# Branch products that share a weight split between the token halves, and an output projection of seven half products

## The chip, the cores and the metric

The kernel runs on 1 core of one Trainium2 chip. The metric is the device time of one launch in microseconds, the median of the runs.

## The reference

One encoder layer on 1024 tokens of 1024 features, in float32. What matters here is the chain of products behind the attention branches:

```python
proj = h @ w_in                                  # h = RMSNorm(x)
y_gla = rms_norm(o_gla) * silu(g_r) @ w_o_gla    # branch A
y_swa = o_swa @ w_o_swa                          # branch B
merged = sigmoid(gate_a) * y_gla + sigmoid(gate_b) * y_swa
x = x + merged @ w_out
h2 = rms_norm(x)
gate, up = split(h2 @ w_ffn_in)                  # 2 x 2816 features
x = x + (silu(gate) * up) @ w_ffn_out
```

## The kernel before

Activations are kept with features on the 128 partitions and tokens along the free axis. The 1024 features are eight tiles (KT = 8), and the tokens two halves of 512 (s = 0, 1), so a tile is 128x512 (HT = 512). Every float32 operand of a product is split into a high part h (a rounded copy, made by ACT) and a low part l (the difference, made by DVE); a product is three matmuls, wh by xh, wh by xl and wl by xh. `wunit` loads a weight block of 128x512 and splits it. The raw blocks have four buffers, h and l five each.

Some products run in a form with seven half products instead of eight: sums and differences of quarter blocks of the weight (`comb`) meet sums and differences of the activations (sets called 11, T1, T2, 21, T3, 22, T4), and the seven results are shared out over the four quarters of the output. A `product` is then four feature tiles by three matmuls, 12 in all. Where two results are the sum of a common part and something else, the products run one behind the other into the same PSUM bank, and the common part is copied out in between, or loaded in first by an ACT copy.

The stages, in the order of the program: the projections of the input with gated linear attention; windowed attention; PAIRS, twelve pairs of input projection (among them the output gate r and the branch gates ga and gb) of which five products each are left (`second_rest`); branches A and B with the output projection; the FFN's input product in 22 blocks (`ffn_in`); and its output product.

Around the change:

- `prep_a(s, k)` loads tile k of the attention output o and of r, forms o times silu(r) times a gain and splits it; `prep_b(s, k)` loads and splits a tile of branch B. In PAIRS one `prep_a(0, f)` is issued behind the eviction of the T3 product in each of the first eight pairs.
- `branch_a(s)`, `branch_b(s)` and `out_proj(s)` run for one token half at a time. Each output tile is an `hgroup`: two weight blocks are loaded and split, then 24 matmuls go into one bank. The order is branch_a(0), branch_b(0), branch_a(1), out_proj(0), branch_b(1), out_proj(1), so each weight block is loaded and split once per half. Behind branch B the merged tile is split at once (mh, ml).
- `out_proj` adds the input x, puts the sum x1 to DRAM, scales it by the gain (xg) and adds its square to `acc`; `combos` makes the FFN's activation sets from xg; `out_stats` turns `acc` into the factor of the norm.
- The FFN runs seven products of 12 matmuls in each block. The first (11) goes into a bank Y, is copied out as p1 and is followed in Y by product 21. p1 stays on chip; the first four blocks make theirs ahead of all others.

PE's instructions keep the order of the program in these stages (`manual_schedule`); on ACT, DVE and SP the scheduler's model sets the order, and each engine issues in that order.

Of the kernel before, what the change touches and what calls it, by code (L numbers as in the profile page):

```python
# [8 lines left out]
F32 = mybir.dt.float32  # L9
# [5 lines left out]
P = 128  # L15
# [7 lines left out]
NA = 4  # L23
NB = 7
# [8 lines left out]
def body(tc, i, out):  # L33
    nc = tc.nc
    with ExitStack() as root:
# [789 lines left out]
        bt = bs.enter_context(tc.tile_pool(name="bt", bufs=2))  # L825
# [59 lines left out]
        def second_rest(f):  # L885
# [16 lines left out]
            if f < 8:  # L902
                with tc.issue_after(v.ins):
                    prep_a(0, f)
# [8 lines left out]
        oa, ob, mh, ml = {0: [], 1: []}, {}, {}, {}  # L913

        def btile(tag, dt=F32, bufs=None):
            return bt.tile([P, HT], dt, tag=tag, name=nm(tag), bufs=bufs)

        def split_in(pool, o, name, k):
            return xsplit(pool, f"{name}h{k}", f"{name}l{k}", o)

        def prep_a(s, k):
            o = stage()
            nc.sync.dma_start(out=o, in_=scr["o", k, s])
            r = stage()
            nc.sync.dma_start(out=r, in_=scr[f"r{k}", s])
            sg = btile("sg", bufs=1)
            nc.scalar.activation(sg, r, AF.Sigmoid)
            nc.vector.tensor_tensor(r, r, sg, op=ALU.mult)
            nc.vector.scalar_tensor_tensor(o, o, og[:, k % 2:k % 2 + 1], r, op0=ALU.mult, op1=ALU.mult)
            oa[s].append(split_in(bo, o, "oa", k))  # L930
# [23 lines left out]
        YX = {q: [] for q in ("11", "T1", "T2", "21", "22", "T3", "T4")}  # L954

        def bsplit(pool, tag, src):
            h = pool.tile([P, HT], FR, tag=tag + "h", name=nm(tag + "h"))
            l = pool.tile([P, HT], FR, tag=tag + "l", name=nm(tag + "l"))
            nc.scalar.activation(h, src, AF.Copy)
            nc.vector.tensor_tensor(l, src, h.bitcast(F32), op=ALU.subtract)  # L960
            return h, l

        def combos(k, step):

            b11, b12, b21, b22 = xg[k][0], xg[k][1], xg[k + 4][0], xg[k + 4][1]
            if step == 0:
                YX["11"].append(bsplit(big1, f"b11{k}", b11))
                YX["21"].append(bsplit(big1, f"b21{k}", b21))
            elif step == 1:
                nc.vector.tensor_tensor(b12, b12, b11, op=ALU.subtract)  # L970
                YX["T1"].append(bsplit(big4, f"bt1{k}", b12))
                YX["22"].append(bsplit(big2, f"b22{k}", b22))
                nc.vector.tensor_tensor(b22, b22, b12, op=ALU.subtract)
                YX["T2"].append(bsplit(big2, f"bt2{k}", b22))
                nc.vector.tensor_tensor(b11, b22, b11, op=ALU.subtract)
                nc.vector.tensor_tensor(b21, b21, b22, op=ALU.subtract)
            else:
                YX["T3"].append(bsplit(big3, f"bt3{k}", b11))
                YX["T4"].append(bsplit(big3, f"bt4{k}", b21))
        bms = ExitStack()  # L980
        bm = bms.enter_context(tc.tile_pool(name="bm", bufs=1, side="right"))
        bob = bs.enter_context(tc.tile_pool(name="bob", bufs=1))

        def hgroup(w, u0, ah, al):
            b = mmtile()
# [8 lines left out]
        acc = fi.tile([P, T], F32, tag="acc", name="acc2")  # L994
        def prep_b(s):
            ob[s] = []
            for k in range(KT):
                o = stage()
                nc.sync.dma_start(out=o, in_=scr["b", k, s])
                ob[s].append(split_in(bob, o, "ob", k))  # L1000

        def gate(nme, s):
            g = btile(nme[:2])
# [4 lines left out]
        def branch_a(s):  # L1008

            for m in range(KT):  # L1010
                g = gate(f"ga{m}", s)
                y = hgroup(i["w_oa"], m, [v[0] for v in oa[s]], [v[1] for v in oa[s]])
                nc.vector.tensor_tensor(xg[m][s], y, g, op=ALU.mult)

        def branch_b(s, between=None):
            for m in range(KT):
                if between and m == 3:
                    between()
                g = gate(f"gb{m}", s)
                y = hgroup(i["w_ob"], m, [v[0] for v in ob[s]], [v[1] for v in ob[s]])  # L1020
                nc.vector.tensor_tensor(g, y, g, op=ALU.mult)
                nc.vector.tensor_tensor(g, g, xg[m][s], op=ALU.add)
                h = bm.tile([P, HT], FR, tag=f"mh{m}", name=nm("mh"))
                l = bm.tile([P, HT], FR, tag=f"ml{m}", name=nm("ml"))
                nc.scalar.activation(h, g, AF.Copy)
                nc.vector.tensor_tensor(l, g, h.bitcast(F32), op=ALU.subtract)
                mh[m], ml[m] = h, l

        def out_proj(s):
            a = acc[:, s * HT:(s + 1) * HT]  # L1030
            for j, m in enumerate((0, 4, 1, 5, 2, 6, 3, 7)):
                xr = stage()
                nc.sync.dma_start(out=xr, in_=i["xT"][m, s])
                y = hgroup(i["w_out"], m, mh, ml)
                nc.vector.tensor_tensor(xr, y, xr, op=ALU.add)
                d = scratch(f"x1_{m}_{s}")
                nc.sync.dma_start(out=d, in_=xr)
                scr["x1", m, s] = d
                nc.scalar.activation(xg[m][s], xr, AF.Copy, scale=g2[:, m:m + 1])
                sq = a if j == 0 else stage()  # L1040
                nc.scalar.activation(sq, xr, AF.Square)
                if j:
                    nc.vector.tensor_tensor(a, a, sq, op=ALU.add)
                if s and m > 3:
                    combos(m - 4, 1)
# [5 lines left out]

        with tc.manual_schedule(engines={mybir.EngineType.PE}):
            branch_a(0)
            prep_b(0)
            for k in range(KT):
                prep_a(1, k)
            branch_b(0)
            branch_a(1)
            prep_b(1)
            out_proj(0)  # L1060
            branch_b(1, lambda: out_stats(0))
        bs.close()
        bigs = ExitStack()
        big1 = bigs.enter_context(tc.tile_pool(name="big1", bufs=1))
        big4 = bigs.enter_context(tc.tile_pool(name="big4", bufs=1))
        big2 = bigs.enter_context(tc.tile_pool(name="big2", bufs=1))
# [6 lines left out]
        home = {"a": ("01", "11", "21", "31", "41", "51", "61", "71"),  # L1073
                "p1": ("01", "11"), "g0": ("41", "51"), "p5": ("00", "10"), "u2": ("20", "30"),
# [25 lines left out]
        def p11(f):  # L1100
            F = feats[f]
            F.Y = mmtile()
            if f < NB:
                w = wunit(i["w_fi"][f, 0])
            else:
                F.r11 = rload(f, 11)
                w = wsplit(F.r11, 512)
            product(F.Y, w, YX["11"], 4, True, False)
            F.p1 = ctile("a" if f < NA else "p1")
            nc.scalar.copy(F.p1, F.Y)  # L1110

        def p21(f):
            F = feats[f]
            w = wunit(i["w_fi"][f, 1]) if f < NB else wsplit(F.r12, 512)
            product(F.Y, w, YX["21"], 4, False, True)
            F.g0 = gate0(F.Y, "a" if f < NA else "g0")

        def ffn_in(f, between):
            F = feats[f]
            if f < NB:  # L1120
                F.r11 = rload(f, 11)
# [12 lines left out]
            for p, g in between:  # L1134
                p(g)
# [96 lines left out]
        with tc.manual_schedule(engines={mybir.EngineType.PE}):  # L1232
            for k in range(4):
                combos(k, 0)
            out_proj(1)
            bms.close()
            big3 = bigs.enter_context(tc.tile_pool(name="big3", bufs=1))

            for f in range(NA):
                if f == NA - 1:  # L1240
                    out_stats(1)
                p11(f)
            for f in range(NA - 1):
                p21(f)
            for k in range(4):
                combos(k, 2)
# [144 lines left out]
```

## Time and profile before

| | us |
|---|---|
| median of 3 runs | 1661.62 (1661.51 to 1662.61) |
| the profiled execution's own time | 1661.65 |
| its span | 1659.9 |
| PE busy | 1639.9 |
| DVE busy | 1183.5 |
| ACT busy | 894.1 |
| PAIRS, from 600.0 to 764.2 | 164.2 |
| branches and projection, to 1026.2 | 262.0 |
| FFN input, from 1046 to 1445 | 399.0 |

PE is TensorE's matmuls and PEld its weight loads, which overlap; DVE is the vector engine, ACT the scalar engine, SP the queue that issues the DMAs. A row of the timeline gives start, duration, engine, line, operation and output <- inputs, and in brackets the idle time before it with what ended it. A line L71 is line 71 of the kernel. In the rows `st` is a staging buffer, `mm` and `ch` are PSUM banks (four of each), wr, wr2 and ws are raw or combined weight blocks, wh and wl their split parts.

### The profile page before, as it was taken

What the parts mean: (1) busy time and instruction counts of PE and PEld (TensorE: products, weight loads), DVE (VectorE), ACT (ScalarE), POOL (GpSimd) and SP (SyncE); (2) the same over time, 40 slices, a digit from 0 to 9 for tenths busy, and PEclk for the clock granted to TensorE, in tenths of its full rate; (3) what the DMA queues carried; (4) which work ended last, traced back from release to release, by engine and by line L of the source; (5) the groups of instructions that cost most, each with busy time, mean ns of one, the idle gap of its engine ahead of it and who ended that gap; (6) DMA issues with size and microseconds to landing.
All of it is one profiled execution on the core that took longest, in us unless ns stands there. A gap on an engine that the chain in (4) does not pass through costs nothing.

```text
span 1659.9 us, 23330 instructions
## 1 busy us (share of the span) xinstructions
PE 1639.9 (99%) x7740; PEld 1361.7 (82%) x7740; DVE 1183.5 (71%) x2276; ACT 894.1 (54%) x1827; POOL 0.2 (0%) x4
## 2 busy tenths in 40 slices
PE   9999999999999999999999999999999999999999
PEld 7888888887888778888888888888888888888887
DVE  8568787846899677654764569766667767679655
ACT  7456776863988754434554456433344434444442
POOL 0000000000000000000000000000000000000000
PEclk9999999999999999999999999999999999999999
DMA  8856757878543486546764545343234443595533
GB/s 278 293 165 206 238 188 241 270 268 289 186 134 108 127 287 214 189 147 221 218 209 141 189 133 165 115 165 102 89 111 157 152 141 132 193 322 189 146 98 119
DMA packets 185993, 304.37 MB, mean 183 GB/s; under 512 B 21166, under 2 KB 46638, under 8 KB 185872
## 3 DMA queue, kind: packets, MB, share of 16 engines
q1 hardware_dynamic: 185872, 302.88, 55.7%
q8 instruction: 61, 1.00, 0.2%
q14 instruction: 60, 0.49, 0.1%
HBM read 206.33 MB, written 96.47 MB: 182 GB/s over the span
## 4 chain that ended last, share of the span: by engine, by line
PE 84%; DVE 6%; ACT 4%; DMA 4%; issue 2%; SPq 0%; DVEq 0%; ACTq 0%
PE mm L75 29%; PE mm L1209 7%; PE mm L853 7%; PE mm L854 7%; PE mm L855 7%; PE ch L75 7%; PE ch L1209 5%; PE ch L853 3%; PE ch L854 3%; PE ch L855 3%; PE mm L245 3%; PE ch L760 1%; DVE wl L71 1%; DMA st<-r 1%; ACT p L743 1%
## 5 line engine op out<-in xcount | busy, mean ns | idle before, releaser
L832 ACT ACTIVATE wh<-ws 128x512 fp32r<-128x512 f32 x136 | 85.6, 631 | 161.2 <-PE ch L854 68.5
L69 ACT ACTIVATE wh<-wr 128x512 fp32r<-128x512 f32 x190 | 118.3, 627 | 96.3 <-PE mm L75 77.3
L71 DVE TENSOR_TENSOR wl<-wr,wh 128x512 fp32r<-128x512 f32 x190 | 130.1, 686 | 38.1 <-ACT wh L69 35.4
L75 PE MATMUL mm<-wh,xh 128*128 128x512 f32 x320 | 127.3, 398 | 0.1
L75 PE MATMUL mm<-wh,xl 128*128 128x512 f32 x320 | 127.1, 397 | 0.0
L75 PE MATMUL mm<-wl,xh 128*128 128x512 f32 x320 | 126.6, 396 | 0.0
L833 DVE TENSOR_TENSOR wl<-ws,wh 128x512 fp32r<-128x512 f32 x136 | 93.4, 686 | 42.5 <-ACT wh L832 42.5
L832 ACT ACTIVATE wh<-a 128x512 fp32r<-128x512 f32 x66 | 41.7, 632 | 93.1 <-PE mm L1209 43.0
L832 ACT ACTIVATE wh<-wr 128x512 fp32r<-128x512 f32 x64 | 40.4, 631 | 85.5 <-PE ch L854 42.4
L833 DVE TENSOR_TENSOR wl<-a,wh 128x512 fp32r<-128x512 f32 x66 | 45.5, 691 | 43.1 <-ACT wh L832 41.0
L1209 PE MATMUL mm<-hh,wh 128*128 128x512 f32 x176 | 68.6, 390 | 0.7 <-DVE c L1148 0.7
L1209 PE MATMUL mm<-hl,wh 128*128 128x512 f32 x176 | 68.5, 389 | 0.0
L1209 PE MATMUL mm<-hh,wl 128*128 128x512 f32 x176 | 68.5, 389 | 0.0
L75 PEld LDWEIGHTS mm<-wl,xh 128*128 128x128 f32 x320 | 60.2, 188 | 9.8
L75 PEld LDWEIGHTS mm<-wh,xl 128*128 128x128 f32 x320 | 60.2, 188 | 9.7
L75 PEld LDWEIGHTS mm<-wh,xh 128*128 128x128 f32 x320 | 60.3, 188 | 9.4 <-ACT st L220 0.3
L846 DVE TENSOR_TENSOR ws<-wr,wr 128x512 f32<-128x512 f32 x68 | 46.7, 689 | 13.5 <-DMA wr<-in_w_fi_dram 10.3
L1182 DVE TENSOR_TENSOR hl<-hr,hh 128x512 fp32r<-128x512 f32 x77 | 52.8, 687 | 4.2 <-ACT hh L1181 4.2
L1209 PE MATMUL ch<-hh,wh 128*128 128x512 f32 x132 | 51.3, 389 | 0.0
L1209 PE MATMUL ch<-hl,wh 128*128 128x512 f32 x132 | 51.3, 389 | 0.0
L1209 PE MATMUL ch<-hh,wl 128*128 128x512 f32 x132 | 51.3, 389 | 0.0
L1181 ACT ACTIVATE hh<-hr 128x512 fp32r<-128x512 f32 x77 | 47.5, 618 | 6.8 <-PE mm L1209 3.9
(542 smaller groups left out, 4934.9 us busy)
## 6 DMA issues: line engine op xcount, KB each, us to landing
wr<-in_w_fi_dram SPq DMA_DIRECT2D x102, 256.0 KB, 2.9
wr<-in_w_f_dram SPq DMA_DIRECT2D x88, 256.0 KB, 3.5
wh<-wh SPq DMA_DIRECT2D x80, 256.0 KB, 3.0
wl<-wl SPq DMA_DIRECT2D x80, 256.0 KB, 2.9
B<-c SPq DMA_DIRECT2D x44, 256.0 KB, 2.1
T<-st SPq DMA_DIRECT2D x44, 256.0 KB, 2.3
a<-in_w_fo_dram SPq DMA_DIRECT2D x44, 256.0 KB, 5.3
hr<-T SPq DMA_DIRECT2D x44, 256.0 KB, 2.7
```

The costliest lines, as they stand in the source:

```text
L69: nc.scalar.activation(h, raw, AF.Copy)
L71: nc.vector.tensor_tensor(l, raw, h.bitcast(F32), op=ALU.subtract)
L75: nc.tensor.matmul(o, a, b, start=start, stop=stop)
L245: nc.tensor.matmul(Y[q], w[:, c], x, start=f0, stop=f1, skip_group_check=True)
L832: nc.scalar.activation(h, src, AF.Copy)
L833: nc.vector.tensor_tensor(l, src, h.bitcast(F32), op=ALU.subtract)
L853: nc.tensor.matmul(o, h[:, c], x[kk][0], start=start and kk == 0, stop=False, skip_group_check=True)
L854: nc.tensor.matmul(o, h[:, c], x[kk][1], start=False, stop=False, skip_group_check=True)
L855: nc.tensor.matmul(o, l[:, c], x[kk][0], start=False, stop=kk == nk - 1, skip_group_check=True)
L1181: nc.scalar.activation(h, r, AF.Copy)
L1182: nc.vector.tensor_tensor(l, r, h.bitcast(F32), op=ALU.subtract)
L1209: nc.tensor.matmul(ys[m], a[:, c], b, start=f0, stop=f1, skip_group_check=True)
```

## The change

- `both(w, m, x)` replaces `hgroup` in branches A and B: one split of each weight block serves both token halves, 48 matmuls into two banks.
- All 16 `prep_a` move into PAIRS (`PREPS`: one or two per pair), all 16 `prep_b` into branch A.
- The order of output tiles in B is 0, 4, 1, 5, ..., and behind each second one `merge(k)` forms the projection's activation sets (YM) from the merged tiles. The sets live in the buffers S0 to S6, which later hold the FFN's sets (YX).
- The output projection is four pairs of seven half products. `out_first(k)` runs product 11 into a bank, has ACT copy it to pt, and runs product 21 into the same bank. `out_open`, `out_go` and `out_rest` run the other five.
- The FFN's first products of all 22 blocks are made ahead (`fill_p`), three in each `out_rest`, ten behind them. Each result p1 is put to DRAM, and `ffn_in` loads it again and copies it into both of its banks.

PE's order in the output projection, first before (the middle of one output tile; mh and ml are the split merged tiles):

```order
L75 MATMUL mm_2694_11532<-mh_2635_11295,wh_2696_11535 128x512
L75 MATMUL mm_2694_11532<-ml_2636_11296,wh_2696_11535 128x512
L75 MATMUL mm_2694_11532<-mh_2635_11295,wl_2697_11537 128x512
L75 MATMUL mm_2694_11532<-mh_2645_11341,wh_2699_11553 128x512
L75 MATMUL mm_2694_11532<-ml_2646_11342,wh_2699_11553 128x512
L75 MATMUL mm_2694_11532<-mh_2645_11341,wl_2700_11555 128x512
```

and after (the end of product 11 and the start of product 21 in `out_first(0)`; S0 and S3 are sets):

```order
L850 MATMUL mm_2509_10939<-S0h3_2499_10915,wh_2511_10942 128x512
L851 MATMUL mm_2509_10939<-S0l3_2500_10916,wh_2511_10942 128x512
L852 MATMUL mm_2509_10939<-S0h3_2499_10915,wl_2512_10944 128x512
L850 MATMUL mm_2509_10939<-S3h0_2417_10427,wh_2515_10962 128x512
L851 MATMUL mm_2509_10939<-S3l0_2418_10428,wh_2515_10962 128x512
L852 MATMUL mm_2509_10939<-S3h0_2417_10427,wl_2516_10964 128x512
```

In both the bank stays the same where the weight block changes; after, the copy of the bank by ACT (pt) lies between the third and the fourth row, and no other product does.

ACT's queue around these copies (pt), after; wh is a split weight block, st a staging buffer:

```order
L67 ACTIVATE wh_2565_11134<-wr_2564_11132 128x512
L1030 COPY pt_2528_11016<-mm_2524_10997 128x512
L67 ACTIVATE wh_2569_11154<-wr_2568_11152 128x512
L1042 COPY mm_2550_11105<-pt_2513_10958 128x512
L1016 ACTIVATE xg10_9594<-st_2532_11036,g2_389 128x512
L1019 ACTIVATE st_2533_11042<-st_2532_11036 128x512
L829 ACTIVATE wh_2589_11223<-ws_2588_11221 128x512
L1030 COPY pt_2544_11076<-mm_2540_11057 128x512
```

and before, in the same stage:

```order
L69 ACTIVATE wh_2752_11795<-wr_2751_11793 128x512
L1039 ACTIVATE xg11_9502<-st_2716_11636,g2_389 128x512
L1041 ACTIVATE st_2724_11679<-st_2716_11636 128x512
L69 ACTIVATE wh_2755_11813<-wr_2754_11811 128x512
L959 ACTIVATE bt11h_2734_11729<-xg11_9502 128x512
L69 ACTIVATE wh_2767_11857<-wr_2766_11855 128x512
```

Before, ACT has no copy of a bank here; after, one stands right behind a weight split.

SP's queue at a double prep, before (o5 and r5 belong to one `prep_a`, ga is a branch gate that is put to DRAM):

```order
L923 DMA st_2053_8732<-o5_0_513 128x512
L116 DMA ga5_1_8730<-st_2052_8728 128x512
L925 DMA st_2054_8734<-r5_0_8275 128x512
L841 DMA wr_2148_9123<-in_w_f_dram 128x512
L841 DMA wr_2149_9125<-in_w_f_dram 128x512
```

and after:

```order
L920 DMA st_2053_8729<-o5_0_513 128x512
L114 DMA ga5_1_8727<-st_2052_8725 128x512
L922 DMA st_2054_8731<-r5_0_8272 128x512
L920 DMA st_2058_8741<-o6_0_515 128x512
L838 DMA wr_2163_9156<-in_w_f_dram 128x512
L922 DMA st_2059_8743<-r6_0_8401 128x512
L838 DMA wr_2164_9158<-in_w_f_dram 128x512
```

The second prep's two loads stand ahead of and between the next weight loads.

DVE's queue at the end of the projection, after (S are the FFN's sets, the last `wl` rows belong to the blocks that `fill_p` makes behind the last pair):

```order
L1010 TENSOR_TENSOR st_2743_11970<-mm_2697_11748,st_2743_11970 128x512
L782 TENSOR_TENSOR S4l3_2776_12056<-xg30_9598,S4h3_2775_12055 128x512
L782 TENSOR_TENSOR S5l3_2784_12072<-xg71_9607,S5h3_2783_12071 128x512
L782 TENSOR_TENSOR S6l0_2786_12076<-xg40_9600,S6h0_2785_12075 128x512
L1021 TENSOR_TENSOR acc2_9620<-acc2_9620,st_2744_11976 128x512
L782 TENSOR_TENSOR S3l3_2751_12003<-xg70_9606,S3h3_2750_12002 128x512
L782 TENSOR_TENSOR S6l1_2788_12080<-xg50_9602,S6h1_2787_12079 128x512
L993 TENSOR_TENSOR xg70_9606<-xg70_9606,ty_2752_12007 128x512
L782 TENSOR_TENSOR S6l2_2790_12084<-xg60_9604,S6h2_2789_12083 128x512
L69 TENSOR_TENSOR wl_2801_12119<-wr_2799_12115,wh_2800_12117 128x512
```

and before:

```order
L1035 TENSOR_TENSOR st_2773_11898<-mm_2774_11900,st_2773_11898 128x512
L71 TENSOR_TENSOR wl_2813_12061<-wr_2811_12057,wh_2812_12059 128x512
L960 TENSOR_TENSOR bt30l_2824_12124<-xg00_9499,bt30h_2823_12123 128x512
L1043 TENSOR_TENSOR acc2_9521<-acc2_9521,st_2781_11941 128x512
L960 TENSOR_TENSOR b223l_2785_11950<-xg71_9514,b223h_2784_11949 128x512
L960 TENSOR_TENSOR bt40l_2826_12128<-xg40_9507,bt40h_2825_12127 128x512
L973 TENSOR_TENSOR xg71_9514<-xg71_9514,xg31_9506 128x512
L71 TENSOR_TENSOR wl_2817_12083<-wr_2815_12079,wh_2816_12081 128x512
```

After the last eviction (L1010, before L1035) the next weight split stands nine rows down instead of one; the splits of sets come first.

The counts change by these rows: PE 7356 to 7308 instructions (48 matmuls), DVE 2271 to 2287, ACT 1644 to 1649, SP 1292 to 1304. The core of the diff:

```diff
-            if f < 8:
-                with tc.issue_after(v.ins):
-                    prep_a(0, f)
+            with tc.issue_after(v.ins):
+                for _ in range(PREPS[f]):
+                    prep_a(*divmod(next(todo_a), KT))
...
+        PREPS = (1, 1, 1, 1, 1, 2, 1, 2, 1, 2, 2, 1)
...
+        def both(w, m, x):
+            b = [mmtile(), mmtile()]
             for u in range(2):
-                h, l = wunit(w[u0, u])
+                h, l = wunit(w[m, u])
                 for kk in range(4):
                     k = u * 4 + kk
                     c = slice(kk * P, (kk + 1) * P)
-                    mm3(b, h[:, c], l[:, c], ah[k], al[k], k == 0, k == KT - 1)
+                    st, sp = k == 0, k == KT - 1
+                    for s in range(2):
+                        mm(b[s], h[:, c], x[s][k][0], st, False)
+                        mm(b[s], h[:, c], x[s][k][1], False, False)
+                    for s in range(2):
+                        mm(b[s], l[:, c], x[s][k][0], False, sp)
             return b
...
+        def merge(k):
+            x11, x12, x21, x22 = xg[k][0], xg[k][1], xg[k + 4][0], xg[k + 4][1]
+            YM["11"].append(xset(HOME["11"], k, x11))
+            YM["21"].append(xset(HOME["21"], k, x21))
+            sub(x12, x12, x11)
+            YM["T1"].append(xset(HOME["T1"], k, x12))
+            sub(x12, x22, x12)
+            YM["T2"].append(xset(HOME["T2"], k, x12))
+            sub(x11, x12, x11)
+            sub(x21, x21, x12)
...
+        def out_first(k):
+            Y = mmtile()
+            product(Y, wunit(i["w_out"][k, 0]), YM["11"], 4, True, True)
+            p = bt.tile([P, HT], F32, tag=("ga", "gb")[k % 2], name=nm("pt"))
+            nc.scalar.copy(p, Y)
+            pt.append(p)
+            product(Y, wunit(i["w_out"][k, 1]), YM["21"], 4, False, True)
+            t = stage()
+            residual(t, Y, k, 0)
+            x1_out(t, k, 0)
...
+        def out_rest(k):
+            g = outs[k]
+            X, Z = g.X, g.Z
...
+            product(X, wsplit(s2, 512), YM["T2"], 4, False, True)
+            u2 = xntile()
+            residual(u2, X, k, 1)
+            fill_p(1)
+            s4 = comb(r12, s2, ALU.subtract)
+            product(Z, wsplit(s4, 512), YM["22"], 4, False, True)
+            nc.vector.tensor_tensor(u2, Z, u2, op=ALU.add)
+            x1_out(u2, k, 1)
+            s3 = comb(g.r11, g.r21, ALU.subtract)
+            product(X, wsplit(s3, 512), YM["T3"], 4, False, True)
+            nc.vector.tensor_tensor(p5, X, p5, op=ALU.add)
+            x1_out(p5, k + 4, 1)
+            fill_p(1)
+            if k < 3:
+                out_open(k + 1)
+                out_go(k + 1)
+            product(X, wsplit(g.r22, 512), YM["T4"], 4, False, True)
...
+            fill_p(1)
+            sums(k)
...
+            for k in range(4):
+                YM["T3"].append(xset(HOME["T3"], k, xg[k][0]))
+                out_first(k)
+                if k == 2:
+                    out_open(0)
+                YM["22"].append(xset(HOME["22"], k, xg[k + 4][1]))
+                YM["T4"].append(xset(HOME["T4"], k, xg[k + 4][0]))
+            out_go(0)
...
+            fill_p(3)
+            out_stats(0)
+            fill_p(2)
+            out_stats(1)
+            fill_p(NFF)
...
-        def ffn_in(f, between):
+        def ffn_in(f):
             F = feats[f]
-            if f < NB:
-                F.r11 = rload(f, 11)
-            F.r12, F.r21, F.r22 = (rload(f, q) for q in (12, 21, 22))
-            p1 = F.p1
-            Z, X = chtile((P, HT)), mmtile()
+            p1 = ctile("p1")
+            nc.sync.dma_start(out=p1, in_=scr["p1", f])
+            F.r11, F.r12, F.r21, F.r22 = (rload(f, q) for q in (11, 12, 21, 22))
+            Z, X, F.Y = chtile((P, HT)), mmtile(), mmtile()
             nc.scalar.copy(X, p1)
+            nc.scalar.copy(F.Y, p1)
```

More of the change, by code (lines that the diff above doesn't have):

```diff
@@ L22 @@
 NFF = 22
-NA = 4
-NB = 7
 WARM = 10
@@ L1006, in gate @@
             return g
[L1008 to L1027, printed above, removed]
@@ L1029, in out_proj @@
-        def out_proj(s):
-            a = acc[:, s * HT:(s + 1) * HT]
[L1031 to L1045, printed above, removed]
+        spare = [(wq, "wr2", 3)] * 3 + [(wq, "ws", 4)] * 4 + [(xn, "xn", 3)]
@@ new lines, in prep_b @@
+        def prep_b(s, k):
+            o = stage()
+            nc.sync.dma_start(out=o, in_=scr["b", k, s])
+            n = 2 * s + k // 4
+            if n < 3:
+                ob[s].append(xset(4 + n, k % 4, o))
+                return
+            h, l = (pool.tile([P, HT], FR, tag=tag, name=nm("ob"), bufs=bufs)
+                    for pool, tag, bufs in (spare.pop(0), spare.pop(0)))
+            nc.scalar.activation(h, o, AF.Copy)
+            nc.vector.tensor_tensor(l, o, h.bitcast(F32), op=ALU.subtract)
+            ob[s].append((h, l))
@@ new lines, in body, with residual, x1_out @@
+        acc = fi.tile([P, T], F32, tag="acc", name="acc2")
+        def residual(d, bank, m, s):
+            nc.sync.dma_start(out=d, in_=i["xT"][m, s])
+            nc.vector.tensor_tensor(d, bank, d, op=ALU.add)
+        done = [False, False]
+        def x1_out(t, m, s):
+            put(("x1", m, s), t)
+            nc.scalar.activation(xg[m][s], t, AF.Copy, scale=g2[:, m:m + 1])
+            a = acc[:, s * HT:(s + 1) * HT]
+            sq = stage() if done[s] else a
+            nc.scalar.activation(sq, t, AF.Square)
+            if done[s]:
+                nc.vector.tensor_tensor(a, a, sq, op=ALU.add)
+            done[s] = True
@@ new lines, in body, with out_open @@
+        pt = []
+        def out_first(k):
[8 more added lines that the diff above has]
+            x1_out(t, k, 0)
+        outs = [Chunk() for _ in range(4)]
+        def out_open(k):
+            g = outs[k]
+            g.X = mmtile()
+            nc.scalar.copy(g.X, pt[k])
+            w = i["w_out"]
+            g.r11, g.r21 = rawload(w[k, 0], True), rawload(w[k + 4, 0], True)
+            g.r22 = rawload(w[k + 4, 1], False)
+            g.s1 = comb(g.r21, g.r22, ALU.add)
+            g.w = wsplit(g.s1, 512)
@@ L1047, in out_stats, with sums @@
+        TY = []
+        def sums(k):
+            b11, b12, b21, b22 = xg[k][0], xg[k][1], xg[k + 4][0], xg[k + 4][1]
+            YX["21"].append(xset(HOME["21"], k, b21))
+            sub(b12, b12, b11)
+            t = bt.tile([P, HT], F32, tag=("ga", "gb")[k % 2], name=nm("ty"))
+            TY.append(t)
+            sub(t, b22, b12)
+            sub(b11, t, b11)
+            sub(b21, b21, t)
         def out_stats(s):
@@ L1065, in body, with fill_p @@
-        big4 = bigs.enter_context(tc.tile_pool(name="big4", bufs=1))
-        big2 = bigs.enter_context(tc.tile_pool(name="big2", bufs=1))
+        ahead = iter(range(NFF))
+        def fill_p(n):
+            for f in [f for _, f in zip(range(n), ahead)]:
+                Y = mmtile()
+                product(Y, wunit(i["w_fi"][f, 0]), YX["11"], 4, True, True)
+                t = stage()
+                nc.scalar.copy(t, Y)
+                put(("p1", f), t)
+        with tc.manual_schedule(engines={mybir.EngineType.PE}):
+            for m in range(KT):
+                g = [gate(f"ga{m}", s) for s in range(2)]
+                y = both(i["w_oa"], m, oa)
+                for s in range(2):
+                    nc.vector.tensor_tensor(xg[m][s], y[s], g[s], op=ALU.mult)
+                for n in (2 * m, 2 * m + 1):
+                    prep_b(*divmod(n, KT))
+            for m in (0, 4, 1, 5, 2, 6, 3, 7):
+                g = [gate(f"gb{m}", s) for s in range(2)]
+                y = both(i["w_ob"], m, ob)
+                for s in range(2):
+                    nc.vector.tensor_tensor(g[s], y[s], g[s], op=ALU.mult)
+                    nc.vector.tensor_tensor(xg[m][s], g[s], xg[m][s], op=ALU.add)
+                if m > 3:
+                    merge(m - 4)
+            for k in range(4):
[6 more added lines that the diff above has]
+            out_go(0)
+            for k in range(4):
+                YX["11"].append(xset(HOME["11"], k, xg[k][0]))
+            for k in range(4):
+                out_rest(k)
+            for q in ("T1", "T2", "T3", "22", "T4"):
+                for k in range(4):
+                    src = {"T1": xg[k][1], "T2": TY[k], "T3": xg[k][0], "22": xg[k + 4][1], "T4": xg[k + 4][0]}[q]
+                    YX[q].append(xset(HOME[q], k, src))
+            fill_p(3)
[3 more added lines that the diff above has]
+            fill_p(NFF)
+            fis.close()
+            hp = x1ss.enter_context(tc.tile_pool(name="hp", bufs=2, side="right"))
@@ L1133, in ffn_in @@
             nc.scalar.copy(u2, X)
-            for p, g in between:
-                p(g)
+            p21(f)
             s3 = comb(F.r11, F.r21, ALU.subtract)
```

124 lines of the change are left out of this document (33 added, 91 removed).

## The prediction

> **What bounds the kernel now.** I read the page's busy line and the shares of its chain first, then the busy time by stage, then the waits of PE, then the chain.
>
> ```profile
> PE 1639.9 (99%) x7740; PEld 1361.7 (82%) x7740; DVE 1183.5 (71%) x2276; ACT 894.1 (54%) x1827; POOL 0.2 (0%) x4
> ...
> PE 84%; DVE 6%; ACT 4%; DMA 4%; issue 2%; SPq 0%; DVEq 0%; ACTq 0%
> ```
>
> PE works 99% of the span, so time leaves only with matmuls or with the few microseconds in which PE stands. The stages (start and end, length, then busy time and count of PE, weight load, DVE, ACT and POOL, the granted clock, DMA share, GB/s):
>
> ```profile
> 372.80:600.00 227.20, 220.38 (x1129) 183.81 (x1128) 186.67 (x541) 166.83 (x394) 0.00 (x0) 0.99 0.56 179
> 600.00:764.20 164.20, 162.49 (x714) 133.45 (x713) 102.86 (x155) 73.13 (x130) 0.00 (x0) 1.00 0.59 193
> 764.20:1026.20 262.00, 262.00 (x1156) 216.62 (x1155) 167.44 (x264) 136.58 (x229) 0.00 (x0) 1.00 0.60 189
> 1046.00:1445.00 399.00, 398.77 (x1760) 329.98 (x1759) 277.17 (x441) 159.16 (x273) 0.00 (x0) 1.00 0.40 134
> ```
>
> They are windowed attention, the PAIRS products, branches with output projection, and FFN input. In the third, which the change rewrites, PE has no idle time at all: 262.00 of 262.00 us. Among PE's waits (total, times, longest) two lie in PAIRS and one at the FFN's end:
>
> ```profile
> PE mm L853 <- ACT nt L895: 0.8, 1, 0.8
> PE mm L853 <- DVE st L862: 0.8, 1, 0.8
> ...
> PE mm L1209 <- DVE c L1148: 0.7, 1, 0.7
> ```
>
> The chain through the rewritten stage is PE alone:
>
> ```profile
> 764.21 189.50 PE mm L75 x836
> 954.56 70.52 PE mm L75 x311
> ```
>
> 189.50 / 836 = 0.2267 us is the pace of one matmul here. Removed weight splits, weight loads or evictions are thus worth nothing by themselves.
>
> **The change part by part.**
>
> *Matmuls.* The projection was 16 blocks of 24, or 384. Now it is 4 pairs x 7 half products x 12 = 336. Branches A and B keep 2 x 384, the FFN its count (the 22 first products move forward, 12 matmuls each). So 48 go, all on the path: 48 x 0.2267 = -10.9 us. The Trainium skill (TensorE: Matmul & The Clock Gate, section Back-to-back issue gap) gives N/2.4 + 2.5 ns for one matmul by itself, 215.8 ns at 512 columns; by it the term would be -10.4 us. The trace has 226.7 ns, and the trace decides.
>
> *Half the weight splits in A and B* (64 blocks to 32), with 4 fewer in the projection: the groups of 764 to 1046 us are
>
> ```profile
> L71 DVE TENSOR_TENSOR wl<-wr,wh 128x512 fp32r<-128x512 f32 x100 | 68.4, 685 | 23.5 <-ACT wh L69 23.5
> L69 ACT ACTIVATE wh<-wr 128x512 fp32r<-128x512 f32 x100 | 62.0, 626 | 61.8 <-PE mm L75 56.0 <-PE mm L854 3.2 <-issue 1.7
> ```
>
> ACT waits here for buffers that PE frees: the splits run ahead of PE. PE never waits for them, so 0.
>
> *Four new waits of PE.* In out_first the second product adds into the bank that holds the first, and ACT must copy the first out in between; PE's order has nothing there. The trace has every part of this:
>
> ```profile
> 620.34 0.57 ACT L895 COPY nt<-mm 128x512 f32<-128x512 f32 x1
> 620.95 0.50 PE L853 MATMUL mm<-xh,wh 128*128 128x512 f32 x1 [0.80 <-ACT nt L895]
> 622.45 0.39 PE L853 MATMUL mm<-xh,wh 128*128 128x512 f32 x1
> ...
> 1434.30 0.39 PE L855 MATMUL mm<-bt23h,wl 128*128 128x512 f32 x1
> 1434.73 0.59 ACT L1133 COPY u<-mm 128x512 f32<-128x512 f32 x1 [1.84 <-PE mm L855]
> ```
>
> An idle ACT starts 0.43 after the last matmul's start (1434.30 to 1434.73), copies for 0.57, and PE follows 0.04 later (620.34 + 0.57 to 620.95). That is 1.04 instead of 0.23, a loss of 0.81. The six matmuls after the wait take 1.50 (620.95 to 622.45) instead of 1.36, another 0.14. So 0.95 each, 3.8 for four.
>
> The copy can stand late in ACT's queue. For pairs 1 and 2 a weight split stands right ahead of it, whose buffer (there are five) comes free with the product that has just ended. The trace has that order:
>
> ```profile
> 754.57 0.39 PE L855 MATMUL mm<-t2h,wl 128*128 128x512 f32 x1
> 754.77 0.63 ACT L69 ACTIVATE wh<-wr 128x512 fp32r<-128x512 f32 x1 [1.61 <-PE mm L854]
> 755.31 0.57 ACT L895 COPY nt<-mm 128x512 f32<-128x512 f32 x1
> ```
>
> The copy starts 0.74 after the last matmul's start instead of 0.43: +0.3 each. For pair 0, splits of S3 and S5 stand ahead; they wait for the last sums of B, at most four DVE operations on two banks, which take 0.60 each:
>
> ```profile
> 1447.00 0.69 DVE L1145 TENSOR_TENSOR u<-u,rstd 128x512 f32<-128x512 f32 x1
> 1447.60 0.69 DVE L1148 TENSOR_TENSOR c<-mm,g 128x512 f32<-128x512 f32 x1
> ```
>
> These are ready at 0.43 + 4 x 0.60 = 2.8 after B's last matmul, the two splits at about 4.0 of ACT time, against 2.5 + 0.43 for the copy; the first split can run after two of the four, which leaves +0.3 to +1.1; I take +0.4. Pair 3: +0.1. Together +4.9. The lower end is 0 (if something covers them), the upper 8.8 (2.2 each: two more operations of 0.5 to 0.7 ahead of every copy).
>
> *The end of the projection.* Before the second fill after the last pair DVE has to clear its queue: from the eviction of the third pair's T3 product to the weight split of FFN block 13 stand 48 operations, 48 x 0.60 = 28.8 us back to back, and PE has 12 products until it needs that split, 144 x 0.2267 = 32.6 us, 33.1 to its third matmul. But nine of them stand behind the last eviction (T4 of the last pair ends ten products on, at 27.2): 0.43 + 0.69 for it, then on ACT a scale of 0.72, two of 0.52, and from there DVE's split, difference and splits at 0.60 and more: 33.6. So +0.5; bounds 0 and 3 (48 x 0.69 = 33.1, plus the waits). The scale's row:
>
> ```profile
> L1039 ACT ACTIVATE xg<-st,g 128x512 f32<-128x512 f32 x16 | 11.6, 723 | 7.5 <-DVE st L1035 7.5
> ```
>
> *PAIRS with 16 preps instead of 8, four of them double.* Before, one pair (60 matmuls) and a prep's loads and chain:
>
> ```profile
> 655.70:669.30 13.60, 13.60 (x61) 11.27 (x61) 9.39 (x15) 6.14 (x11) 0.00 (x0) 1.00 0.60 199
> ...
> st<-r SPq DMA_DIRECT2D x8, 256.0 KB, 4.5
> ...
> ACT sg L927 <- DMA st<-r: 17.6, 8, 4.1
> ...
> 617.76 0.69 DVE L928 TENSOR_TENSOR st<-st,sg 128x512 f32<-128x512 f32 x1 [2.91 <-ACT sg L927]
> ```
>
> DVE is idle for 13.6 - 9.4 = 4.2 us a pair. A second prep adds three operations (1.9) and a second wait as at 617.76 (2.9): 0.6 too many. A T3 eviction may be late by 2.72 - 1.17 = 1.55, since one product (12 x 0.2267) lies between it and T4, and it takes 0.43 + 0.69 + 0.05. So no stall: 0. Bounds: -1.6 (both waits shown above vanish) and +4 (1 us per double).
>
> *A and B.* The first group of A needs its last set only at its 45th matmul, 2.7 + 44 x 0.2267 = 12.7 us after the last T3; eviction 1.1, load 4.5 and a chain of about 4 make 9.6. B's sets are formed during A at two per 10.9 us. The projection's last S3 set: 3.8 against 5.0 and more. All 0.
>
> *FFN.* p1 comes by a load and one more ACT copy per block, and the product of r11 leaves. A late block before:
>
> ```profile
> 1383.00:1402.00 19.00, 19.00 (x86) 15.73 (x85) 13.83 (x22) 7.60 (x14) 0.00 (x0) 1.00 0.37 129
> ```
>
> After, 72 matmuls take 16.3 us, DVE 21 x 0.63 = 13.2 (81%, was 73%), ACT 15 x 0.54 = 8.1. The Y bank is opened two products ahead of its use. The block's last evictions still end in the wait of 0.7 on L1148: 0, with -0.7 (gone) to +0.6 (one DVE operation more) as bounds.
>
> Sum: -10.9 + 4.9 + 0.5 = -5.5. The profiled execution took 1661.65 (span 1659.9), 0.03 above the median 1661.62: 1661.6 - 5.5 = 1656.1 us.
>
> **The rivals.** A measurement here tells about 0.2% from no change, 3.3 us: 1658.3 and 1665.0.
>
> *ACT and DVE are late everywhere*: junctions 2.2 each, 2.5 at block 13. -10.9 + 8.8 + 2.5 = +0.4: 1662.0. For it: the projection puts evictions, squares, splits and set forming on both engines where before PE had 24-matmul groups. Against: halved splits in A and B let them start ahead.
>
> *The junctions are free*, since something stands between after all: 1656.1 - 4.9 = 1651.2. Against it PE's order.
>
> *Slower: the double preps hold PE.* The r loads queue behind puts that free their buffers, and every microsecond beyond a wait of 2.9 + 0.95 (the slack of 1.55 less 0.6) is a microsecond of T4. To pass 1665.0 each of the four must cost 8.9 / 4 = 2.2, so a DVE wait near 6 us; with 6.5 us in each it ends at 1666.7. The longest wait of ACT there is 4.1, for one prep, which speaks against it; the DMA share of 0.59 speaks for it.
>
> *Slower: the clock.* Should the granted clock halve over the four junctions, their 96 matmuls cost 0.2267 more each, 21.8: 1677.9. The windowed attention row speaks against: with 6.8 us of PE idle it kept 0.99. The Trainium skill (the same page, section A second HAM failure mode: psum-queue depth-cycling) says that short PE pauses between matmul groups can make the gate swing between half and full rate, and its section What's actually happening puts the drop behind an idle window of about 3.4 us. By the first this rival would hold, by the second not, and the trace agrees with the second so far.
>
> **How the numbers follow.** Forecast 0.60 (its own range 1653.0 to 1658.3); late everywhere 0.22; free junctions 0.07; double preps 0.07; clock 0.04. Faster 0.67, same 0.22, slower 0.11. The range leaves out the two slower cases and the last of the free one: 1651.2 to 1662.4.
>
> **What would show it.** PE with 48 matmuls fewer. Four waits of PE for ACT's copy pt of 0.8 to 1.3 us, and one for the split of block 13. No PE wait in PAIRS beyond the two of 0.8, none in A, B and the rest of the projection, FFN blocks at 16.3 us, a clock of 1.00. Junction waits over 1.5, or waits at the fills, would mean that I took ACT's or DVE's queue too lightly; waits on T4 in PAIRS would mean the same for the preps.

## The result, and the profile after

The changed kernel takes 1652.89 us in the median of 4 runs (1651.37 to 1654.16), against 1662.11 (1661.51 to 1663.0) for the kernel before: a ratio of 0.9947 (95% interval 0.9934 to 0.9959), faster by 9.2 us. A second measurement, the first experiment below, gives 1653.55 against 1660.45, ratio 0.9956 (0.9942 to 0.997), 6.9 us. The forecast was 1656.1, 5.5 us faster, in a range of 1651.2 to 1662.4.

The profiled execution took 1654.16 with a span of 1652.4, 7.5 us less than the span before. The busy line of its page:

```profile
PE 1630.3 (99%) x7692; PEld 1351.9 (82%) x7692; DVE 1192.7 (72%) x2292; ACT 895.7 (54%) x1832; POOL 0.2 (0%) x4
```

PE has 48 matmuls fewer (7740 to 7692), DVE 16 instructions more (2276 to 2292) and ACT 5 more (1827 to 1832): the profile counts otherwise than the list of the change, but finds the same differences. The waits of PE over the span, shortened to those from PAIRS on (total, times, longest):

```profile
PE mm L850 <- ACT pt L1030: 3.7, 4, 1.0
...
PE mm L852 <- DVE wl L69: 0.6, 1, 0.6
...
PE mm L1278 <- DVE c L1217: 0.4, 1, 0.4
...
PE mm L850 <- ACT nt L892: 0.3, 1, 0.3
...
PE mm L850 <- DVE st L859: 0.2, 1, 0.2
```

The first is the four junctions (a junction is the place where product 21 follows product 11 in the same bank and waits for the copy pt), the second the weight split of FFN block 13; both stand in the forecast. The third was 0.7 before, at the FFN's end. The last two are of the kinds that took 0.8 each in PAIRS before. The first junction on PE and on ACT, with the seventh matmul of product 21:

```profile
938.39 0.39 PE L852 MATMUL mm<-S0h,wl 128*128 128x512 f32 x1
939.64 0.50 PE L850 MATMUL mm<-S3h,wh 128*128 128x512 f32 x1 [0.87 <-ACT pt L1030]
941.14 0.39 PE L850 MATMUL mm<-S3h,wh 128*128 128x512 f32 x1
...
938.49 0.63 ACT L781 ACTIVATE S5h<-xg 128x512 fp32r<-128x512 f32 x1
939.02 0.57 ACT L1030 COPY pt<-mm 128x512 f32<-128x512 f32 x1
```

PE's next matmul starts 1.25 after the last one instead of 0.23, and six matmuls take 1.50 instead of 1.36. The copy starts 0.63 after the last matmul's start, since the split of S5 stands ahead of it. The idle times of the four are 0.87, 0.97, 0.97 and 0.86. The profile counts a matmul of 0.39 as busy, although the next could follow 0.23 after its start, so 0.16 has to be added to each, and 0.14 for the slower restart: the four cost 4.9 us.

Two matmuls mark off the rewritten stretch: the last of the PAIRS products and the first of the FFN's output product. Before, then after:

```profile
763.82 0.39 PE L855 MATMUL mm<-xh,wl 128*128 128x512 f32 x1
...
1445.41 0.39 PE L1209 MATMUL mm<-hh,wh 128*128 128x512 f32 x1
```

```profile
762.50 0.39 PE L852 MATMUL mm<-xh,wl 128*128 128x512 f32 x1
...
1438.38 0.39 PE L1278 MATMUL mm<-hh,wh 128*128 128x512 f32 x1
```

681.59 us became 675.88: -5.7. The remaining 1.8 of the span's 7.5 lie outside: 1.3 up to the first mark and 0.5 behind the second.

### The profile page after: what moved, and what is told of

The parts are those of the page before. It is cut to its first block, busy times and chain, and to the rows that moved or that the text cites. A ratio compares the mean times of both kernels' runs of the same rounds, so it can differ in the third digit from the quotient of the medians.

```text
span 1652.4 us, 23247 instructions
## 1 busy us (share of the span) xinstructions
PE 1630.3 (99%) x7692; PEld 1351.9 (82%) x7692; DVE 1192.7 (72%) x2292; ACT 895.7 (54%) x1832; POOL 0.2 (0%) x4
## 5 line engine op out<-in xcount | busy, mean ns | idle before, releaser
L829 ACT ACTIVATE wh<-ws 128x512 fp32r<-128x512 f32 x152 | 95.9, 631 | 182.5 <-PE mm L851 103.6
L67 ACT ACTIVATE wh<-wr 128x512 fp32r<-128x512 f32 x142 | 88.7, 628 | 105.2 <-PE mm L73 58.5
L69 DVE TENSOR_TENSOR wl<-wr,wh 128x512 fp32r<-128x512 f32 x142 | 97.3, 688 | 47.3 <-ACT wh L67 46.7
L830 DVE TENSOR_TENSOR wl<-ws,wh 128x512 fp32r<-128x512 f32 x152 | 104.2, 686 | 18.9 <-ACT wh L829 18.7
L843 DVE TENSOR_TENSOR ws<-wr,wr 128x512 f32<-128x512 f32 x76 | 52.3, 689 | 6.4 <-DMA wr<-in_w_f_dram 2.6
L829 ACT ACTIVATE wh<-wr 128x512 fp32r<-128x512 f32 x60 | 37.8, 629 | 31.4 <-ACT mm L1194 13.2
```

Source lines behind the costliest of these rows:

```text
L67: nc.scalar.activation(h, raw, AF.Copy)
L69: nc.vector.tensor_tensor(l, raw, h.bitcast(F32), op=ALU.subtract)
L843: nc.vector.tensor_tensor(t, x, y, op=op)
```

## Experiments

The experiments ran on three chips, on each beside the kernel before. Where a stretch is given, it is the one between the two marks, which leaves out what scatters ahead of it.

**The changed kernel again.** No edit.

> The changed kernel again, unaltered, to see how its executions scatter and where. Theory (the sum of the prediction holds for like executions): where an execution shows the same granted clock as one of the kernel before, it is 6 to 8 us shorter; the first four executions fell into two pairs, 1651.4 and 1652.0 at a clock of 1.000, 1653.8 and 1654.2 at 0.998, and both clocks will be seen again, some 2 us apart. Rival (the change itself saves 9 us, and the profiled execution was a slow one of it): the kernel before shows the same two clocks and yet stays 9 us above at each.

1653.55 (1652.57 to 1654.54, 5 runs) against 1660.45 (1658.22 to 1663.13, 9 runs). Over all runs whose clock was recorded, the medians of before and after at 1.000 are 1658.99 (8 runs) and 1651.95 (3), at 0.999 they are 1660.53 (18) and 1653.99 (4), at 0.998 they are 1662.07 (13) and 1654.00 (2): 7.0, 6.5 and 8.1 us. That is about the theory's 6 to 8, and less than the rival's 9. The two clocks did not come again as forecast: one of these five runs has 1.000, four have 0.999 and none has 0.998.

The stretch is 676.34, 0.5 longer than in the first profile. The waits for pt explain it: they are 0.85, 0.97, 0.97 and 1.33, since the weight block that DVE's queue takes ahead of the fourth junction landed later (DVE idles 3.24 for it instead of 2.24), and with it the operations of DVE and ACT ahead of that copy. The four junctions cost 5.3 here.

**Interleaved first products.**

```diff
-            for k in range(4):
-                YM["T3"].append(xset(HOME["T3"], k, xg[k][0]))
-                out_first(k)
+            for k in (0, 2):
+                for j in (k, k + 1):
+                    YM["T3"].append(xset(HOME["T3"], j, xg[j][0]))
+                    out_11(j)
+                out_21(k)
...
+                out_21(k + 1)
```

> Products 11 of two pairs run one behind the other into two banks, then their products 21: each copy of a bank by ACT now has a whole product of 2.7 us beside it. Theory (the four waits for the copy pt are real losses of 1.2 us each, 0.87 to 0.97 of idle and the slow restart): 4.9 us shorter than the changed kernel, no wait for pt. Rival (PE would have waited a little later anyway, for the sets or for the splits): the pt waits go but come back as waits of the following products, under 2 us shorter.

`out_11` is product 11 with the copy, `out_21` the rest of `out_first`; the forming of the sets for products 22 and T4 moves behind both products 21.

1649.51 (1649.05 to 1650.06), 4.0 us under the changed kernel on the same chip, without overlap of the runs. The waits of PE behind the first 598 us:

```profile
PE mm L1287 <- DVE c L1226: 1.1, 1, 1.1
PE mm L850 <- ACT wh L829: 0.7, 1, 0.7
PE mm L852 <- DVE wl L69: 0.6, 1, 0.6
```

No wait for pt is left. The stretch is 671.07 (761.99 to 1433.06), 5.3 under the run above and 4.8 under the first profile: what the junctions cost in each of them, 5.3 and 4.9. The wait for wh lies in PAIRS, that of 1.1 behind the second mark; they may be why the whole time shows less than the stretch. The junctions were a loss on the path, and an avoidable one.

**The split of block 13 earlier.**

```diff
+            fill_p(3)
             for q in ("T1", "T2", "T3", "22", "T4"):
                 ...
-            fill_p(3)
```

> The three FFN first products behind the last pair are written ahead of the 20 splits of the FFN's sets, so that DVE makes the weight split of block 13 earlier; nothing else is moved. Theory (DVE's queue of splits is what PE waits 0.6 us for): that wait goes, 0.7 to 0.9 us shorter, and since ten products lie before the first use of the sets no new wait comes. Rival (the sets are late in turn): a wait of about the same size at the first FFN block, no change in the time.

1654.23 (1653.56 to 1654.75), 0.7 above the changed kernel and within its scatter. The stretch is 675.01, 0.9 and 1.3 under the two profiles of the changed kernel, and the wait for wl is gone with no new one up to the FFN's end. Its junctions wait as long as those of the first profile (3.6 and 3.7 in total), so the 0.9 is the comparison to go by. The theory holds for the stretch, but this execution reached PAIRS 1.5 us later than the first profile (598.45 against 596.94), and the run times can't resolve 0.9 us.

**Both edits.**

> Both edits, the interleaved first products and the early splits. Theory: their gains add, 5.6 to 5.8 us shorter than the changed kernel, so about 1647 us in the median, with no wait of PE from the start of branch A to the end of the FFN's input. Rival: with PE 4.9 us earlier at the end of the projection DVE's queue is late by more than the early split gives back, 3 to 4.5 us shorter only.

1648.90 (1645.13 to 1650.38), ratio to before 0.9925 (0.9912 to 0.9939): the fastest of all versions, though its runs overlap those of the interleaving alone. From 590 us to the end PE has one wait:

```profile
PE mm L850 <- ACT nt L892: 0.3, 1, 0.3
```

It lies in PAIRS. The stretch is 670.18 (763.74 to 1433.92), 5.7 and 6.2 under the changed kernel: the gains add. The median is only 4.7 under that of the changed kernel, short of the 5.6 to 5.8 forecast and of 1647; the rival's late queue isn't the reason, since PE has no wait in the stretch.

**Weight blocks split twice.**

```diff
-                h, l = wunit(w[m, u])
+                hl = [wunit(w[m, u]) for _ in range(2)]
...
-                        mm(b[s], h[:, c], x[s][k][0], st, False)
+                        mm(b[s], hl[s][0][:, c], x[s][k][0], st, False)
```

> In branches A and B each weight block is loaded and split twice again, once for each token half, as in the kernel before; all else is as changed. Theory (the splits were hidden before and are hidden now): the same time as the changed kernel within 0.5 us, 32 more splits of ACT and of DVE, no new wait of PE. Rival (the saved splits are what lets ACT and DVE keep up with the sets): waits for sets or for the copies at the end of branch B, 2 to 8 us longer.

1654.34 (1652.5 to 1655.55), ratio 0.9957 (0.9942 to 0.9972), as the changed kernel. The stretch is 676.68, 0.3 and 0.8 above; branches A and B take 173.40 us up to the first matmul of the projection, as in the profile after (762.50 to 935.89). So the splits saved there were worth nothing in time. Only the wait for block 13's split grew:

```profile
PE mm L850 <- ACT pt L1030: 3.7, 4, 1.0
PE mm L852 <- DVE wl L69: 1.2, 1, 1.2
```

Nine operations ahead of that split, DVE waits 0.58 for the load of the residual x (oc<-x); in the first profile it had no pause there. Whether the added weight loads delayed it was not tried.

**A repeated product in each junction.**

```diff
-            product(Y, wunit(i["w_out"][k, 0]), YM["11"], 4, True, True)
+            w11 = wunit(i["w_out"][k, 0])
+            product(Y, w11, YM["11"], 4, True, True)
...
             pt.append(p)
+            product(chtile((P, HT)), w11, YM["11"], 4, True, True)
             product(Y, wunit(i["w_out"][k, 1]), YM["21"], 4, False, True)
```

> Between product 11 and product 21 of each of the four pairs product 11 is run once more into a spare bank whose content is not used: 48 matmuls come back, and cover the copy. Theory (a matmul costs 0.2267 us here, and a junction 1.2 us): 48 x 0.2267 - 4.9 = 6.0 us longer than the changed kernel, no wait for pt. Rival (the junctions cost nothing by themselves): 10.9 longer.

1660.34 (1657.39 to 1665.25, 10 runs), ratio to before 0.9995 (0.9985 to 1.0005). The stretch is 681.91 (759.98 to 1441.89), 6.0 above the first profile of the changed kernel and 5.6 above the second, with no wait for pt. That is 10.9 for the 48 matmuls less the 4.9 and 5.3 that the junctions cost in those profiles; the rival's 10.9 are off by five.

**Doubles in a row.** `PREPS = (1, 1, 1, 1, 2, 2, 2, 2, 2, 2, 0, 0)`.

> The preps of branch A's inputs stand in PAIRS as 1, 1, 1, 1, 2, 2, 2, 2, 2, 2, 0, 0: six doubles in a row. Theory (a double costs nothing while DVE's wait for r stays under 3.9 us): PAIRS within 1 us of the changed kernel. Rival (the loads of r queue behind the puts, T4 waits for the late eviction): 1 to 2 us per double, 6 to 12 us longer.

1656.16 (1654.4 to 1658.49), ratio 0.997 (0.9958 to 0.9981), some 2 us above the changed kernel's 0.9956. From the first PAIRS matmul to the first mark it is 166.8 us (595.61 to 762.41) against 165.56 and 164.85. Waits of PE in PAIRS:

```profile
PE mm L850 <- ACT nt L892: 0.9, 2, 0.7
PE mm L850 <- DVE st L859: 0.4, 1, 0.4
```

Neither fits well. The wait for st comes at 609.77, ahead of the first double. The two for nt, at 700.28 and 714.85, lie among the doubles; with the 0.30 of each wait from above they cost 1.5 us, so six doubles in a row aren't free, but cost some 0.25 us each. Nor does T4 wait there for a late eviction, as the rival has it. The copy nt is late on ACT, where the activation of the second prep's r (L924) stands ahead of it; before the wait at 714.85 that activation itself waits 0.70 for the load of r.

**Fours.** `PREPS = (1, 1, 1, 1, 4, 4, 4, 0, 0, 0, 0, 0)`.

> The preps stand in PAIRS as 1, 1, 1, 1, 4, 4, 4 and none after. By the prediction's account of DVE three more preps add 9 operations, 5.7 us, to a pair in which DVE is idle for 4.2 us, besides one wait of about 2.9 us or more for r: the eviction of T3 is late by 4.4 us less the slack of 1.55, near 3 us for each of the three pairs, 8 to 10 us longer. Rival (the operations run ahead and are spread over the following pairs, which have no prep): under 2 us longer.

1670.19 (1667.36 to 1674.94), ratio 1.0056 (1.0038 to 1.0075): 0.6% slower than before. PAIRS takes 179.07, 13.5 more than in the profile after, and more than the 8 to 10 forecast; the stretch behind it is unchanged (675.90). The waits of PE from 598 to 785 us, and DVE's queue at the first of the three, with the last T1 matmul ahead of it and the first T4 matmul:

```profile
PE mm L850 <- DVE st L859: 11.7, 3, 5.8
...
679.39 0.39 PE L852 MATMUL ch<-xh,wl 128*128 128x512 f32 x1
682.85 0.50 PE L850 MATMUL mm<-xh,wh 128*128 128x512 f32 x1 [3.07 <-DVE st L859]
...
678.26 0.68 DVE L843 TENSOR_TENSOR ws<-wr,ws 128x512 f32<-128x512 f32 x1
679.04 0.69 DVE L782 TENSOR_TENSOR S1l<-st,S1h 128x512 fp32r<-128x512 f32 x1
679.65 0.68 DVE L925 TENSOR_TENSOR st<-st,sg 128x512 f32<-128x512 f32 x1
680.25 0.68 DVE L859 TENSOR_TENSOR st<-ch,nt 128x512 f32<-128x512 f32 x1
680.85 0.74 DVE L926 SCALAR_TENSOR_TENSOR st<-st,og,st 128x512 f32<-128x512 f32 x1
681.51 0.68 DVE L830 TENSOR_TENSOR wl<-ws,wh 128x512 fp32r<-128x512 f32 x1
682.11 0.69 DVE L859 TENSOR_TENSOR st<-mm,nt 128x512 f32<-128x512 f32 x1
```

DVE works without a pause, the preps' operations (L925, L926, L782) among the others, and the eviction of T3 (the last row) comes 3 us after T1 has ended: T4 waits for it. This is the slower rival of the prediction, by its mechanism. Its three waits are 3.07, 5.80 and 2.84, a mean of 3.9 where the account of DVE gave 3. Behind the longest of them the granted clock falls (0.57 from 702 to 706 us), which the account doesn't have either; the runs longer than the profiled one show lower clocks too, 0.996 at 1669.70 and 1670.68, 0.993 at 1674.94. The changed kernel stays ahead of the point from which this wait decides: no pair of it has more than two preps, and in neither profile of it does PE wait in a pair with two.

**The kernel before again.** No edit.

> The kernel before, unaltered, with a second profile, to see how much of the difference ahead of branch A belongs to the change. In the first profile PAIRS took 166.6 us to the start of its last T4 matmul; six profiles of the changed kernel or of edits outside PAIRS have 164.8 to 165.8. Theory (the waits of PE for T3's eviction and for the copies in PAIRS follow the landing of the loads of r and scatter from execution to execution): PAIRS of this profile lies between 164.8 and 167, and the stretch from that matmul to the FFN's output product at 681.6 us within 0.6. Rival (the change takes about 1.2 us out of PAIRS, by another order of the queues there): 166.4 to 166.8 again, with the same two waits of 0.8.

1660.45 (1659.07 to 1662.95, 8 runs), ratio 0.9998 (0.9987 to 1.0009). Its second profile has one wait in PAIRS:

```profile
PE mm L853 <- ACT nt L895: 0.5, 1, 0.5
```

PAIRS takes 165.43 (596.28 to 761.71), in the middle of the changed kernel's 164.8 to 165.8, and the stretch 682.02 (to 1443.73), 0.4 above the first profile. Of the two waits of 0.8 the one for T3's eviction is gone, the one for the copy nt has come again at 0.5. So the shorter PAIRS of the first profile after isn't shown to be the change's doing.

In both profiles before the stretch has one wait, in the FFN's first block, and it accounts for the 0.4; first the profile before, then this one:

```profile
1059.04 0.50 PE L853 MATMUL mm<-bt40h,wh 128*128 128x512 f32 x1 [0.23 <-DVE c L1139]
```

```profile
1057.36 0.50 PE L853 MATMUL mm<-bt40h,wh 128*128 128x512 f32 x1 [0.66 <-DVE c L1139]
```

## Why the prediction was right

By its own terms:

- *Matmuls, -10.9.* 48 fewer by the count, at 0.2267 each; the repeated products put 48 back and cost 10.9 less the junctions.
- *Halved splits, 0.* Splitting twice again changed nothing up to the projection; the stretch is 0.3 to 0.8 longer, which is mostly the later split of block 13.
- *Junctions, +4.9.* Measured 4.9 and 5.3 in the two traces, 4.8 and 5.3 by interleaving. The account for the two middle pairs came true: their copies are late by 0.30 and 0.31, the forecast had 0.3 each. For the first and the last it had 0.4 and 0.1, and the first profile has 0.20 and 0.21; that these two misses cancel is luck, and in the second profile the last copy is late by 0.67. The rival of free junctions is wrong, although the first median lies near its 1651.2.
- *The split of block 13, +0.5.* PE waited 0.6; with the gap's other parts it is about 0.85. DVE worked back to back up to that split. The account has ACT's scale and splits in the path there; DVE in fact had no pause from 1037.6 on, and took the last eviction 0.68 after its matmul's start instead of 0.43:

```profile
1047.28 0.69 DVE L1010 TENSOR_TENSOR st<-mm,st 128x512 f32<-128x512 f32 x1
...
1052.69 0.69 DVE L69 TENSOR_TENSOR wl<-wr,wh 128x512 fp32r<-128x512 f32 x1
...
1052.49 0.39 PE L851 MATMUL mm<-S0l,wh 128*128 128x512 f32 x1
1053.44 0.50 PE L852 MATMUL mm<-S0h,wl 128*128 128x512 f32 x1 [0.56 <-DVE wl L69]
```

- *PAIRS, 0.* PE has no wait in a doubled pair, in either profile after. The two profiles of the kernel before differ by 1.2 us in PAIRS.
- *A, B and FFN, 0.* No wait of PE there. From the start of the second norm sum to the second mark it is 373.51 us in the profile after and in every profile of an edit. What the sum left out is the wait in the FFN's first block before, which the prediction doesn't name: with the 0.30 of each wait it cost 0.5 us in the first profile and about 0.9 in the second, and it is in no profile after. Why it went was not tried.

The sum for the stretch is -5.5; the two profiles before (681.59, 682.02) and the two after (675.88, 676.34) give -5.3 to -6.1. With the measured terms the first pair closes: -10.9 for the matmuls, +4.9, +0.85 and -0.5 for the wait that went are -5.65, against -5.7. The forecast's two smaller misses, 0.35 at block 13 and this 0.5, nearly cancel.

The rival with ACT and DVE late everywhere didn't come, since the junctions cost 1.2 each and not 2.2. The clock rival didn't come either: the granted clock stayed at 1.00 in the window of the four junctions, with 3.7 us of PE idle in 26.8:

```profile
935.90:962.70 26.80, 23.13 (x98) 17.90 (x97) 22.02 (x36) 15.45 (x28) 0.00 (x0) 1.00 0.43 146
```

But the prediction set that rival aside by a wrong reading. Its 0.99 for windowed attention is a mean over 227 us; in slices of 4 us (the granted clock is the third number from the end) the same profile has a fall:

```profile
568.00:572.00 4.00, 1.83 (x6) 0.64 (x4) 1.03 (x3) 3.98 (x12) 0.00 (x0) 1.00 0.28 87
572.00:576.00 4.00, 3.66 (x11) 2.75 (x12) 0.69 (x1) 1.27 (x3) 0.00 (x0) 0.58 0.08 20
```

No wait of PE around it is longer than 1.31 us. So the profile before did not speak for the need of a long idle window; it showed short waits close together with a fall behind them. That the junctions did not cause one is measured, but not by the reason that the prediction gives.

What the working has too small is the whole time: 9.2 us in the first measurement and 6.9 in the second, against 5.5. The first median, 1652.89, lies in the range, but just under the forecast's own part of it, 1653.0 to 1658.3. All 45 runs of the kernel before have a median of 1661.08, the 9 of the changed one 1653.55: 7.5 us. The stretch explains 5.3 to 6.1. The rest, about 1.5 to 2 us, would lie ahead of the stretch or behind it, where single executions scatter by 4 us (PAIRS began between 594.1 and 598.5 us). Like clocks don't remove it, and the profiles show no part of it: ahead of PAIRS, in PAIRS and behind the second mark the two kernels' values overlap. The kernel with the repeated products, whose stretch is as long as that of the kernel before, runs 0.8 us shorter than it, with an interval from 2.5 shorter to 0.8 longer. Whether the change has a part in the rest stays open.

## What to carry to other kernels

Fewer matmuls are worth their pace where PE never stops, but the form that saves them brings copies of a bank between two products into it, and each such copy costs about 1.2 us here; with another product in between it cost nothing. Judge a change by the stretch between two marks of one trace: it resolved half a microsecond where the run times of one kernel scattered by two to five. Work moved beside a busy engine was free here with two preps in a pair and cost little with six such pairs in a row; with four preps in a pair the engine in the middle, DVE, delayed the eviction that PE waits for. A mean over a long stage hides a short fall of the clock; look at it in short slices.

## What the hardware showed that had not been expected

The scatter of single executions has one visible source. Near the end of windowed attention PE has short waits in a row, 1.31, 0.22 and 0.75 us in each of the eleven profiles. In ten of them, of both kernels and all edits but one, the granted clock falls there for a few microseconds. Here is the profile after, then the run with the repeated products, the only one without the fall, whose edit lies behind this place:

```profile
568.00:572.00 4.00, 1.82 (x6) 0.63 (x4) 1.03 (x3) 3.98 (x12) 0.00 (x0) 1.00 0.27 83
572.00:576.00 4.00, 3.89 (x12) 2.82 (x13) 0.69 (x1) 1.27 (x4) 0.00 (x0) 0.57 0.07 20
```

```profile
568.00:572.00 4.00, 2.51 (x7) 1.34 (x8) 1.55 (x3) 2.43 (x6) 0.00 (x0) 1.00 0.00 0
572.00:576.00 4.00, 4.00 (x23) 3.29 (x22) 2.49 (x4) 2.30 (x4) 0.00 (x0) 1.00 0.29 88
```

The run without the fall reached PAIRS at 594.1 us, the others between 595.6 and 598.5. The Trainium skill (TensorE: Matmul & The Clock Gate, section What's actually happening) puts the drop behind an idle window of about 3.4 us; here three such waits, 2.3 us of idle in 3.5 us, came with a fall in ten executions and without one in the eleventh, while the four junctions, 6.7 us apart, never lowered the clock. What decides between the executions was not tried.
